# The last output tile of a hybrid trunk: 256 tokens at once, or two halves of 128 with a scale of their own

## The chip, the cores and the metric

The kernel runs on one core of one Trainium2 chip. The metric is the device time of one execution in microseconds. A kernel is run several times, and the median counts.

## The reference

One layer of a trunk for 256 tokens and 2048 features: a gated recurrent branch, a gated short convolution, a merge, then a squared-ReLU MLP and a final RMSNorm. The change touches the MLP and the final norm only:

```
h2 = _rmsnorm(x, g2)
u = jnp.square(jax.nn.relu(jnp.einsum("bsd,df->bsf", h2, w_mlp1)))
x = x + jnp.einsum("bsf,fd->bsd", u, w_mlp2)
...
return _rmsnorm(x, final_g)      # x * rsqrt(mean(x*x) + 1e-6) * g
```

## The kernel before

Everything lies with features on the 128 partitions and tokens along the free axis. The tile `x` is [128, 16, 256]: 16 tiles of 128 features by 256 tokens. Every float32 operand of a matmul is split into two parts of the type fp32r, a high one and a low one, and a product is made of three terms: high weight by high and low activation (one matmul of 512 columns, since the two activation parts lie side by side), and low weight by high activation (one of 256 columns). `product` (L226 on) issues these pairs at L232 and L233, 8 to a slab of weights.

Weights stream in as slabs of [128, 1024]. `Weights.make` loads a slab by a DMA from the SP queue (L61), rounds it on ScalarE into `whi` (L63) and makes `wlo` as the difference on VectorE (L64). `Weights.take` keeps three slabs ahead; four buffers of each kind exist, so the rounding of a slab waits until TensorE is done with the slab four before it.

The MLP has 8192 hidden features and runs in two passes `h` of 4096. In a pass, 32 tiles of `u` are made (L380: squared ReLU, then `split`, L133 and L134), and then 16 output tiles, each of 4 slabs, or 32 pairs (L387 on). The second RMSNorm is not applied ahead of the first matrix: its factor `rs` (1 / mean square, since the ReLU is squared) multiplies the output tiles at L389. In the second pass each tile is also squared and added to `ssq` (`squares`, L190 and L191) and multiplied by the final gain (L395).

The last tile of the second pass (`flat`) has three matmuls of 256 columns per row block in place of the pair (L228 to L230), all into one half of a PSUM tile, so that no addition of two halves follows. Then come L389 and L390, the squares of this tile (L397), the gain (L398), and `rsqrt` (L156): two matmuls with a matrix of ones (L154) put the sum over features on every partition, for 256 tokens; ScalarE takes a square root (L161), VectorE a reciprocal (L164) and one Newton step (L165 to L167), all on [128, 256]. Six products (L403) scale the 16 tiles, and after each a DMA (L404) stores [128, n, 256], on the SP queue or on ScalarE's.

Each engine works its instructions in the order in which they are issued; a framework inserts the semaphores.

Of the kernel before, what the change touches and what calls it, by code (L numbers as in the profile page):

```python
# [14 lines left out]
P = 128  # L15
# [9 lines left out]
AHEAD = 300  # L25

PARAMS = [("g1", NT), ("g2", NT), ("gf", NT), ("b_in", 7 * NT), ("ca_w", 4 * NT), ("ca_b", NT),
          ("br", NT), ("bi", NT), ("lam", NT), ("cb_w", 3 * NT), ("one", 1)]
OFF = {}
_n = 0  # L30
for _name, _w in PARAMS:
# [5 lines left out]


class Weights:
    """Streams [128, ncol] slabs of weights and splits each exactly into two fp32r parts."""  # L40

    def __init__(self, tc, raw_pool, hi_pool, lo_pool, slabs):
        self.tc, self.nc, self.slabs = tc, tc.nc, slabs
# [41 lines left out]
def trunk(ctx: ExitStack, tc: tile.TileContext, xT, par, w_in, w_lru, w_pa, w_pb, w_o, w_1, w_2, out):  # L85
# [43 lines left out]
        return pr[:, OFF[name] + j:OFF[name] + j + 1]  # L129

    def split(dst, src):
        """dst [P, 2, S] fp32r <- src as two parts."""
        nc.scalar.copy(dst[:, 0, :], src)  # L133
        nc.vector.tensor_tensor(dst[:, 1, :], src, dst[:, 0, :].bitcast(F32), ALU.subtract)  # L134

# [12 lines left out]
    ssq = keep.tile([P, S], F32, name="ssq")  # L148

    def total(parts):  # L150
        """PSUM [P, S]: the sum over partitions and parts, on every partition."""
        ps = psl.tile([P, 512], F32, name="psl")
        for i, sq in enumerate(parts):
            nc.tensor.matmul(ps[:, :S], ones, sq, start=i == 0, stop=i == len(parts) - 1)  # L154
        return ps[:, :S]

    def rsqrt(dst, parts):
        """dst [P, S] <- 1 / sqrt(mean of the squares + EPS)."""
        ps = total(parts)
        y = wk.tile([P, S], F32, name="t")  # L160
        nc.scalar.activation(y, ps, AF.Sqrt, scale=1.0 / D, bias=eps)  # L161
        m = wk.tile([P, S], F32, name="low")
        nc.vector.tensor_scalar(m, ps, 1.0 / D, EPS, ALU.mult, ALU.add)
        nc.vector.reciprocal(y, y)  # L164
        nc.vector.tensor_tensor(m, m, y, ALU.mult)  # L165
        nc.vector.scalar_tensor_tensor(m, m, -0.5, y, ALU.mult, ALU.mult)
        nc.vector.scalar_tensor_tensor(dst, m, 1.5, y, ALU.add, ALU.mult)  # L167
# [14 lines left out]
    nc.sync.dma_start(pr[:, NT:], par[:, NT:])  # L182

    def squares(src, j):
        """ssq, by partition, of the tiles up to j."""
        if j == 0:
            nc.scalar.activation(ssq, src, AF.Square)
        else:
            sq = wk.tile([P, S], F32, name="s")
            nc.scalar.activation(sq, src, AF.Square)  # L190
            nc.vector.tensor_tensor(ssq, ssq, sq, ALU.add)  # L191
# [5 lines left out]
    s2 = keep.tile([P, NT], F32, name="s2")  # L197

    def decay():
        """s4 <- -4 softplus(-lam)."""  # L200
        nc.scalar.activation(s2, lam, AF.Abs)
        nc.scalar.activation(sg, s2, AF.Sigmoid, scale=-1.0)
        nc.vector.tensor_scalar(sd, sg, -1.0, 2.0, ALU.mult, ALU.add)
        nc.vector.reciprocal(sd, sd)
        nc.vector.tensor_tensor(sg, sg, sd, ALU.mult)
        nc.vector.tensor_tensor(s2, sg, sg, ALU.mult)
        nc.vector.tensor_scalar(sd, s2, 1.0 / 17, 1.0 / 15, ALU.mult, ALU.add)
        for n in (13, 11, 9, 7, 5, 3, 1):
            nc.vector.tensor_tensor(sd, sd, s2, ALU.mult)
            nc.vector.tensor_scalar(sd, sd, 1.0 / n, None, ALU.add)  # L210
        nc.vector.tensor_tensor(sd, sd, sg, ALU.mult)
        nc.vector.tensor_scalar(s2, lam, -1.0, 0.0, ALU.mult, ALU.max)
        nc.vector.scalar_tensor_tensor(s2, sd, 2.0, s2, ALU.mult, ALU.add)
        nc.vector.tensor_scalar(s4, s2, -4.0, None, ALU.mult)

    def product(acts, k0, nh, flat=False):
        """PSUM [P, 2, S]: the sum of its two halves, or if flat its first half, is the next weights' product
        with acts."""
        ps = psz.tile([P, 2, S], F32, name="psz")
        n = nh * HALF  # L220
        for c in range(nh):
            hi, lo = W.take()
            for k in range(HALF):
                a = acts(k0 + c * HALF + k)
                i = c * HALF + k
                if flat:  # L226
                    w = slice(k * P, (k + 1) * P)
                    nc.tensor.matmul(ps[:, 0, :], hi[:, w], a[:, 0, :], start=i == 0, stop=False)  # L228
                    nc.tensor.matmul(ps[:, 0, :], hi[:, w], a[:, 1, :], start=False, stop=False)  # L229
                    nc.tensor.matmul(ps[:, 0, :], lo[:, w], a[:, 0, :], start=False, stop=i == n - 1)  # L230
                    continue
                nc.tensor.matmul(ps, hi[:, k * P:(k + 1) * P], a, start=i == 0, stop=False)  # L232
                nc.tensor.matmul(ps[:, 1, :], lo[:, k * P:(k + 1) * P], a[:, 0, :], start=False, stop=i == n - 1)  # L233
        return ps
# [17 lines left out]
        z_done(z_product(), j, dst, func)  # L252

    def first_pair():
        """The products of the first two tiles, side by side, as x and the weights come in."""
        w = W.first(4)
        two = [psz.tile([P, 2, S], F32, name="psz") for _ in range(2)]
        for k in range(NT):
            for m in range(2):
                hi, lo = w[k // HALF * 2 + m]  # L260
                c = slice(k % HALF * P, (k % HALF + 1) * P)
                nc.tensor.matmul(two[m], hi[:, c], xg[:, k], start=k == 0, stop=False)  # L262
                nc.tensor.matmul(two[m][:, 1, :], lo[:, c], xg[:, k, 0, :], start=False, stop=k == NT - 1)  # L263
        return two
# [109 lines left out]
    for h in range(2):  # L374
        u = [(big2 if h == 1 and c == 0 else big).tile([P, NT, 2, S], F32R, name="mg" if h == 1 and c == 0 else "big")
             for c in range(2)]
        for f in range(NF // 2):
            t = added(product(lambda k: xh[:, k], 0, 2))
            v = wk.tile([P, S], F32, name="s")
            nc.vector.scalar_tensor_tensor(v, t, 0.0, t, ALU.max, ALU.mult)  # L380
            split(u[f // NT][:, f % NT], v)
            if h == 0 and f == 0:
                nc.vector.tensor_scalar(rs, total([ssq]), 1.0 / D, EPS, ALU.mult, ALU.add)
                nc.vector.reciprocal(rs, rs)
        for j in range(NT):
            flat = h == 1 and j == NT - 1
            ps = product(lambda k: u[k // NT][:, k % NT], 0, 4, flat)  # L387
            t = wk.tile([P, S], F32, name="t") if flat else added(ps)
            nc.vector.tensor_tensor(t, ps[:, 0, :] if flat else t, rs, ALU.mult)  # L389
            nc.vector.tensor_tensor(x[:, j, :], x[:, j, :], t, ALU.add)  # L390
            if h == 1 and j < NT - 1:
                squares(x[:, j, :], j)
                if j == NT - 2:
                    nc.scalar.activation(sink, ssq[:, 0:1], AF.Sqrt)
                nc.scalar.activation(x[:, j, :], x[:, j, :], AF.Copy, scale=pc("gf", j))  # L395
    last = wk.tile([P, S], F32, name="s")
    nc.scalar.activation(last, x[:, NT - 1, :], AF.Square)  # L397
    nc.scalar.activation(x[:, NT - 1, :], x[:, NT - 1, :], AF.Copy, scale=pc("gf", NT - 1))  # L398
    rsqrt(rs, [ssq, last])
    at = 0  # L400
    for n in (3, 4, 4, 3, 1, 1):
        c = slice(at, at + n)
        nc.vector.tensor_tensor(x[:, c, :], x[:, c, :], rs1.broadcast_to([P, n, S]), ALU.mult)  # L403
        (nc.sync if at < 3 or at % 2 == 1 and at != 7 else nc.scalar).dma_start(out[:, c, :], x[:, c, :])  # L404
        at += n


def _slabs(w):
    """[K, N] -> [N / 128, K / 1024, 128, 1024]: per 128 columns and 1024 rows, one slab with the rows' low
    index on the partitions."""  # L410
    k, n = w.shape
    w = w.reshape(k // (HALF * P), HALF, P, n // P, P)
    return np.ascontiguousarray(w.transpose(3, 0, 2, 1, 4)).reshape(n // P, k // (HALF * P), P, HALF * P)


def _cols(v):
    """[..., n * 128] -> [128, ... * n]."""
    return np.asarray(v).reshape(-1, P).T


# [28 lines left out]
```

## Time and profile before

| what | value |
|---|---|
| median of 3 runs | 1669.2 us |
| lowest and highest run | 1667.7 and 1669.64 us |
| the profiled execution's span, first to last instruction | 1667.7 us |
| mean granted TensorE clock of the core | 0.996 |
| TensorE busy over the span | 1645.6 us, 99% |
| stores of the output, the two of 384 KB | 2.6 us to landing |

The profiled execution took 1667.7 us, its span, as long as the lowest of the three runs. The views used below are the page of the profile, the timeline (start, length, engine, line, operation, and in brackets the idle time before it and what ended it), the groups of instructions by line and shape, and tables of windows (busy time and number of instructions of each engine in a stretch, then the granted TensorE clock as a share of full speed, the busy share of the 16 DMA engines, and what they moved in GB/s).

### The profile page before, as it was taken

The page shows a single profiled execution, that of the slowest core. Times are in us where ns is not written, and L with a number is a line of the kernel's source. Part 1 is how long each engine was busy: PE and PEld are TensorE (multiplying, and loading weights), DVE is VectorE, ACT ScalarE, POOL GpSimd, SP SyncE. Part 2 cuts the span into 40 slices and gives each one's busy share as a digit, 9 for nine tenths or more (in the row PEclk, how much of TensorE's full clock was granted, in tenths as well). Part 3 has the DMA queues.
Part 4 walks back from the last instruction along what each step waited for, and adds up shares of the span by engine and source line. Part 5 has one row for each costly group of instructions (what it writes and reads, how often), then busy time and mean ns, then how long its engine had stood idle before and what let it go on. Part 6 is the DMA issues. An engine that isn't in the chain of part 4 may idle for free.

```text
span 1667.7 us, 24308 instructions
## 1 busy us (share of the span) xinstructions
PE 1645.6 (99%) x9450; PEld 1437.3 (86%) x9450; DVE 1124.6 (67%) x1617; ACT 866.4 (52%) x1270; POOL 3.4 (0%) x37
## 2 busy tenths in 40 slices
PE   8999999999999999999999999999999999999996
PEld 6888888888888888888888888888888888888886
DVE  7989778878977665656666666665555666655554
ACT  7666666666665444444445544444443444444442
POOL 0000000000000000000000000000000000000000
PEclk9999999999999999999999999999999999999998
DMA  7555555555556555555555555555555555555552
GB/s 256 177 191 188 189 190 189 186 189 189 185 186 191 189 189 188 185 188 188 188 189 189 179 189 189 190 190 189 187 188 185 188 189 188 189 190 190 188 188 93
DMA packets 88244, 312.15 MB, mean 187 GB/s; under 512 B 9920, under 2 KB 12352, under 8 KB 88128
## 3 DMA queue, kind: packets, MB, share of 16 engines
q1 hardware_dynamic: 87840, 309.93, 56.5%
q8 instruction: 74, 1.21, 0.3%
q10 hardware_dynamic: 288, 0.66, 0.1%
q14 instruction: 42, 0.34, 0.1%
HBM read 308.45 MB, written 2.10 MB: 186 GB/s over the span
## 4 chain that ended last, share of the span: by engine, by line
PE 97%; DVE 1%; DMA 1%; ACT 0%; issue 0%; SPq 0%; DVEq 0%; ACTq 0%
PE psz L232 62%; PE psz L233 32%; DMA raw<-w_in_s 1%; PE psz L262 1%; PE psl L327 0%; PE psl L328 0%; PE psl L326 0%; DVE wlo L64 0%; PE psz L263 0%; PE psz L229 0%; PE psz L230 0%; PE psz L228 0%; DVE x L403 0%; ACT whi L63 0%; PE psl L154 0%
## 5 line engine op out<-in xcount | busy, mean ns | idle before, releaser
L232 PE MATMUL psz<-big,whi 128*128 128x512 f32 x4048 | 1420.9, 394 | 1.0 <-ACT whi L63 0.8
L233 PE MATMUL psz<-big,wlo 128*128 128x256 f32 x4048 | 1130.5, 279 | 0.8 <-DVE wlo L64 0.8
L64 DVE TENSOR_TENSOR wlo<-raw,whi 128x1024 fp32r<-128x1024 f32 (+1 forms) x596 | 714.0, 1201 | 511.7 <-ACT whi L63 510.6
L63 ACT CAST whi<-raw 128x1024 fp32r<-128x1024 f32 (+1 forms) x596 | 614.3, 1032 | 772.5 <-issue 433.5
L232 PEld LDWEIGHTS psz<-big,whi 128*128 128x128 f32 x4048 | 759.2, 188 | 182.8 <-ACT whi L63 1.1
L233 PEld LDWEIGHTS psz<-big,wlo 128*128 128x128 f32 x4048 | 759.3, 188 | 1.1 <-DVE wlo L64 1.1
L232 PE MATMUL psz<-mg,whi 128*128 128x512 f32 x496 | 174.6, 395 | 0.0
L233 PE MATMUL psz<-mg,wlo 128*128 128x256 f32 x496 | 139.0, 281 | 0.0
L232 PEld LDWEIGHTS psz<-mg,whi 128*128 128x128 f32 x496 | 93.0, 187 | 22.1 <-DVE mg L134 0.3
L240 DVE TENSOR_TENSOR t<-psz,low 128x256 f32<-128x256 f32 x255 | 105.7, 417 | 0.0
L233 PEld LDWEIGHTS psz<-mg,wlo 128*128 128x128 f32 x496 | 93.7, 189 | 0.0
L238 ACT COPY low<-psz 128x256 f32<-128x256 f32 x255 | 93.1, 365 | 0.0
L245 DVE TENSOR_TENSOR t<-t,rs 128x256 f32<-128x256 f32 x112 | 47.1, 422 | 2.3
L380 DVE SCALAR_TENSOR_TENSOR s<-t 128x256 f32<-128x256 f32 x64 | 27.2, 425 | 2.1
L338 DVE RECIPROCAL q<-q 128x512 f32<-128x512 f32 x8 | 26.8, 3346 | 0.0
L294 DVE SCALAR_TENSOR_TENSOR xc<-xa,pr,xc 128x256 f32<-128x256 f32 x48 | 22.0, 475 | 0.0
L134 DVE TENSOR_TENSOR big<-s,big 128x256 fp32r<-128x256 f32 x48 | 20.1, 419 | 0.0
L262 PE MATMUL psz<-big,whi 128*128 128x512 f32 x32 | 14.0, 478 | 5.7 <-ACT whi L63 5.7
L133 ACT CAST big<-s 128x256 fp32r<-128x256 f32 x48 | 19.3, 402 | 0.0
L327 PE MATMUL psl<-xs,whi 128*128 128x256 f32 x64 | 18.0, 281 | 0.0
L328 PE MATMUL psl<-xs,wlo 128*128 128x256 f32 x64 | 17.9, 280 | 0.0
L326 PE MATMUL psl<-xs,whi 128*128 128x256 f32 x64 | 17.8, 278 | 0.0
(122 smaller groups left out, 529.4 us busy)
## 6 DMA issues: line engine op xcount, KB each, us to landing
raw<-w_s SPq DMA_DIRECT2D x256, 512.0 KB, 3.5
raw<-w_in_s SPq DMA_DIRECT2D x220, 512.0 KB, 4.2
raw<-w_pb_s SPq DMA_DIRECT2D x32, 512.0 KB, 4.2
raw<-w_pa_s SPq DMA_DIRECT2D x32, 512.0 KB, 4.1
raw<-w_o_s SPq DMA_DIRECT2D x32, 512.0 KB, 3.5
raw<-w_lru_s SPq DMA_DIRECT2D x8, 512.0 KB, 4.0
x<-xT SPq DMA_DIRECT2D x8, 256.0 KB, 4.4
raw<-w_in_s SPq DMA_DIRECT2D x16, 128.0 KB, 4.2
```

The costliest lines, as they stand in the source:

```text
L63: nc.scalar.copy(hi[:, c], raw[:, c])
L64: nc.vector.tensor_tensor(lo[:, c], raw[:, c], hi[:, c].bitcast(F32), ALU.subtract)
L134: nc.vector.tensor_tensor(dst[:, 1, :], src, dst[:, 0, :].bitcast(F32), ALU.subtract)
L232: nc.tensor.matmul(ps, hi[:, k * P:(k + 1) * P], a, start=i == 0, stop=False)
L233: nc.tensor.matmul(ps[:, 1, :], lo[:, k * P:(k + 1) * P], a[:, 0, :], start=False, stop=i == n - 1)
L238: nc.scalar.copy(low, ps[:, 1, :])
L240: nc.vector.tensor_tensor(t, ps[:, 0, :], low, ALU.add)
L245: nc.vector.tensor_tensor(t, t, rs, ALU.mult)
L262: nc.tensor.matmul(two[m], hi[:, c], xg[:, k], start=k == 0, stop=False)
L294: nc.vector.scalar_tensor_tensor(c, xa[:, m, tap:tap + S], pc("ca_w", tap * NT + j), c, ALU.mult, ALU.add)
L338: nc.vector.reciprocal(q, q)
L380: nc.vector.scalar_tensor_tensor(v, t, 0.0, t, ALU.max, ALU.mult)
```

## The change

1. The `flat` form is gone from `product`. The last tile is made by `half(th, between)`, once for tokens 0 to 127 and once for 128 to 255. Each half goes through the same four slabs: 32 pairs of one matmul of 2 x 128 columns (high weights; both activation parts) and one of 128 columns (low weights).
2. The scale of each half is made with tokens on partitions. The squares are the stationary operand and one column of ones the moving one, so the sum lands as [128 tokens, 1]; root, reciprocal and Newton step run on one column. To bring it back to all feature partitions, the identity matrix times the scale (a new parameter `eye`, 128 columns more in the second load of `pr`) is multiplied by ones (`spread`).
3. The matmuls for this stand at chosen places among the pairs: the sum over `ssq` after 16 pairs of the first half and after 20 of the second, the first half's scale after 10 pairs of the second half, its `spread` after 22.
4. The output is [2, 128, 16, 128]; stores move [128, n, 128] (runs of 128 floats in `x`), all on the SP queue: 5, 5, 3, 3 tiles of the first half, then 2, 4, 5, 5 of the second.
5. In the second pass `rs` multiplies `v` ahead of `split` (32 times on [128, 256]) in place of the output tiles (16 times).

```
@@ for f in range(NF // 2):
             nc.vector.scalar_tensor_tensor(v, t, 0.0, t, ALU.max, ALU.mult)
+            if h == 1:
+                nc.vector.tensor_tensor(v, v, rs, ALU.mult)
             split(u[f // NT][:, f % NT], v)
...
-        for j in range(NT):
-            flat = h == 1 and j == NT - 1
-            ps = product(lambda k: u[k // NT][:, k % NT], 0, 4, flat)
-            t = wk.tile([P, S], F32, name="t") if flat else added(ps)
-            nc.vector.tensor_tensor(t, ps[:, 0, :] if flat else t, rs, ALU.mult)
+        for j in range(NT - h):
+            t = added(product(lambda k: u[k // NT][:, k % NT], 0, 4))
+            if h == 0:
+                nc.vector.tensor_tensor(t, t, rs, ALU.mult)
             nc.vector.tensor_tensor(x[:, j, :], x[:, j, :], t, ALU.add)
...
-    rsqrt(rs, [ssq, last])
-    for n in (3, 4, 4, 3, 1, 1):
...
+    def sum_of(th):
+        ps = psl.tile([P, 512], F32, name="psl")
+        nc.tensor.matmul(ps[:, 0:1], ssq[:, th * P:(th + 1) * P], ones[:, 0:1], start=True, stop=False)
+        return ps
+
+    def half(th, between):
+        c = slice(th * P, (th + 1) * P)
+        ps = psz.tile([P, 2, S], F32, name="psz")
+        for k in range(4 * HALF):
+            if k in between:
+                between[k]()
+            hi, lo = w[k // HALF]
+            a = u[k // NT][:, k % NT, :, c]
+            b = slice(k % HALF * P, (k % HALF + 1) * P)
+            nc.tensor.matmul(ps[:, :, :P], hi[:, b], a, start=k == 0, stop=False)
+            nc.tensor.matmul(ps[:, 1, :P], lo[:, b], a[:, 0, :], start=False, stop=k == 4 * HALF - 1)
+        low = wk.tile([P, S], F32, name="low")
+        nc.scalar.copy(low[:, :P], ps[:, 1, :P])
+        xl = x[:, NT - 1, c]
+        nc.vector.tensor_tensor(low[:, :P], low[:, :P], xl, ALU.add)
+        nc.vector.tensor_tensor(xl, ps[:, 0, :P], low[:, :P], ALU.add)
+        sq = wk.tile([P, S], F32, name="s")
+        nc.scalar.activation(sq[:, :P], xl, AF.Square)
+        nc.scalar.activation(xl, xl, AF.Copy, scale=pc("gf", NT - 1))
+        return sq
+
+    def scale_of(th, sq):
+        ps = col[th]
+        nc.tensor.matmul(ps[:, 0:1], sq[:, :P], ones[:, 0:1], start=False, stop=True)
+        r, y, m = (keep.tile([P, 1], F32, name="%s%d" % (n, th)) for n in ("cr", "cy", "cm"))
+        nc.scalar.activation(y, ps[:, 0:1], AF.Sqrt, scale=1.0 / D, bias=eps)
...
+        d = wk.tile([P, S], F32, name="t")
+        nc.vector.tensor_scalar(d[:, :P], eye, m, None, ALU.mult)
+        return d
+
+    def spread(d):
+        ps = psl.tile([P, 1, 512], F32, name="psl")
+        nc.tensor.matmul(ps[:, 0, :P], ones, d[:, :P], start=True, stop=True)
+        return ps[:, :, :P]
+
+    def store(th, by, at, parts):
+        for n in parts:
+            xp = x[:, at:at + n, th * P:(th + 1) * P]
+            nc.vector.tensor_tensor(xp, xp, by.broadcast_to([P, n, P]), ALU.mult)
+            nc.sync.dma_start(out[th, :, at:at + n, :], xp)
+            at += n
+
+    s0 = half(0, {2 * HALF: lambda: begin(0)})
+    s1 = half(1, {10: lambda: by.append(scale_of(0, s0)), 20: lambda: begin(1), 22: store0})
+    store(0, by[0], 10, (3, 3))
+    store(1, spread(scale_of(1, s1)), 0, (2, 4, 5, 5))
```

On TensorE (`psz` is the product's PSUM tile, `psl` that of the small sums, `big` the tile of `u`), the program before ends with the last three of the 96 matmuls of the flat tile and the two sums:

```order
L228 MATMUL psz<-big,whi 128x256
L229 MATMUL psz<-big,whi 128x256
L230 MATMUL psz<-big,wlo 128x256
L154 MATMUL psl<-ssq,ones 128x256
L154 MATMUL psl<-s,ones 128x256
L444 UNCONDITIONAL_BRANCH
```

Now the same place, late in the second half, at its pairs 19 to 23:

```order
L412 MATMUL psz<-big,wlo 128x128
L399 MATMUL psl<-ones,ssq 128x1
L411 MATMUL psz<-big,whi 128x2x128
L412 MATMUL psz<-big,wlo 128x128
L411 MATMUL psz<-big,whi 128x2x128
L412 MATMUL psz<-big,wlo 128x128
L441 MATMUL psl<-t,ones 128x128
L411 MATMUL psz<-big,whi 128x2x128
```

The small matmuls, which stood behind the last product, now stand between its pairs for the first half; those of the second half still stand behind.

On VectorE, at the end of the program, before (from the sum of squares of the last tile but one to the scaled products):

```order
L191 TENSOR_TENSOR ssq<-ssq,s 128x256
L389 TENSOR_TENSOR t<-psz,rs 128x256
L390 TENSOR_TENSOR x<-x,t 128x256
L163 TENSOR_SCALAR low<-psl 128x256
L164 RECIPROCAL t<-t 128x256
L165 TENSOR_TENSOR low<-low,t 128x256
L166 SCALAR_TENSOR_TENSOR low<-low,t 128x256
L167 SCALAR_TENSOR_TENSOR rs<-low,t 128x256
L403 TENSOR_TENSOR x<-x,rs 128x768
L403 TENSOR_TENSOR x<-x,rs 128x1024 x2
```

Now, from the four products of the first half on (`cr`, `cy`, `cm` are the columns of the scale, `pr` holds the identity):

```order
L447 TENSOR_TENSOR x<-x,psl 128x5x128 x2
L447 TENSOR_TENSOR x<-x,psl 128x3x128 x2
L416 TENSOR_TENSOR low<-low,x 128x128
L417 TENSOR_TENSOR x<-psz,low 128x128
L429 TENSOR_SCALAR cr_15888<-psl 128x1
L430 RECIPROCAL cy_15889<-cy_15889 128x1
L431 TENSOR_TENSOR cm_15890<-cr_15888,cy_15889 128x1
L432 SCALAR_TENSOR_TENSOR cm_15890<-cm_15890,cy_15889 128x1
L433 SCALAR_TENSOR_TENSOR cm_15890<-cm_15890,cy_15889 128x1
L435 TENSOR_SCALAR t<-pr,cm_15890 128x128
L447 TENSOR_TENSOR x<-x,psl 128x2x128
L447 TENSOR_TENSOR x<-x,psl 128x4x128
```

The first half's products stand ahead of the second half's additions on this engine, and the operations that make the scale are one column wide.

More of the change, by code (lines that the diff above doesn't have):

```diff
@@ L27 @@
 PARAMS = [("g1", NT), ("g2", NT), ("gf", NT), ("b_in", 7 * NT), ("ca_w", 4 * NT), ("ca_b", NT),
-          ("br", NT), ("bi", NT), ("lam", NT), ("cb_w", 3 * NT), ("one", 1)]
+          ("br", NT), ("bi", NT), ("lam", NT), ("cb_w", 3 * NT), ("one", 1), ("eye", P)]
 OFF = {}
@@ L214, in decay, with product @@
         nc.vector.tensor_scalar(s4, s2, -4.0, None, ALU.mult)
-    def product(acts, k0, nh, flat=False):
+    def product(acts, k0, nh):
         ps = psz.tile([P, 2, S], F32, name="psz")
@@ L225, in product @@
                 i = c * HALF + k
[L226 to L231, printed above, removed]
                 nc.tensor.matmul(ps, hi[:, k * P:(k + 1) * P], a, start=i == 0, stop=False)
@@ L384, in trunk @@
                 nc.vector.reciprocal(rs, rs)
-        for j in range(NT):
-            flat = h == 1 and j == NT - 1
-            ps = product(lambda k: u[k // NT][:, k % NT], 0, 4, flat)
-            t = wk.tile([P, S], F32, name="t") if flat else added(ps)
-            nc.vector.tensor_tensor(t, ps[:, 0, :] if flat else t, rs, ALU.mult)
+        for j in range(NT - h):
+            t = added(product(lambda k: u[k // NT][:, k % NT], 0, 4))
+            if h == 0:
+                nc.vector.tensor_tensor(t, t, rs, ALU.mult)
             nc.vector.tensor_tensor(x[:, j, :], x[:, j, :], t, ALU.add)
-            if h == 1 and j < NT - 1:
+            if h == 1:
                 squares(x[:, j, :], j)
@@ L395, in trunk @@
                 nc.scalar.activation(x[:, j, :], x[:, j, :], AF.Copy, scale=pc("gf", j))
-    last = wk.tile([P, S], F32, name="s")
-    nc.scalar.activation(last, x[:, NT - 1, :], AF.Square)
-    nc.scalar.activation(x[:, NT - 1, :], x[:, NT - 1, :], AF.Copy, scale=pc("gf", NT - 1))
-    rsqrt(rs, [ssq, last])
-    at = 0
-    for n in (3, 4, 4, 3, 1, 1):
[L402 to L405, printed above, removed]
+    w = [W.take() for _ in range(4)]
@@ new lines, in trunk @@
+    eye = pr[:, OFF["eye"]:OFF["eye"] + P]
+    col = {}
+    def sum_of(th):
[22 more added lines that the diff above has]
+        return sq
@@ new lines, in scale_of @@
+    def scale_of(th, sq):
[3 more added lines that the diff above has]
+        nc.scalar.activation(y, ps[:, 0:1], AF.Sqrt, scale=1.0 / D, bias=eps)
+        nc.vector.tensor_scalar(r, ps[:, 0:1], 1.0 / D, EPS, ALU.mult, ALU.add)
+        nc.vector.reciprocal(y, y)
+        nc.vector.tensor_tensor(m, r, y, ALU.mult)
+        nc.vector.scalar_tensor_tensor(m, m, -0.5, y, ALU.mult, ALU.mult)
+        nc.vector.scalar_tensor_tensor(m, m, 1.5, y, ALU.add, ALU.mult)
+        d = wk.tile([P, S], F32, name="t")
+        nc.vector.tensor_scalar(d[:, :P], eye, m, None, ALU.mult)
+        return d
@@ new lines, in spread, with begin @@
+    def spread(d):
[8 more added lines that the diff above has]
+            at += n
+    def begin(th):
+        col[th] = sum_of(th)
@@ L408, in _slabs, with store0 @@
+    by = []
+    def store0():
+        by.append(spread(by.pop()))
+        store(0, by[0], 0, (5, 5))
+    s0 = half(0, {2 * HALF: lambda: begin(0)})
+    s1 = half(1, {10: lambda: by.append(scale_of(0, s0)), 20: lambda: begin(1), 22: store0})
+    store(0, by[0], 10, (3, 3))
+    store(1, spread(scale_of(1, s1)), 0, (2, 4, 5, 5))
 def _slabs(w):
@@ L431 @@
         "par": np.ascontiguousarray(np.concatenate([_cols(v) for v in (
-            norm1_g, norm2_g, final_g, b_in, conv_a_w, conv_a_b, lru_br, lru_bi, lru_lam, conv_b_w, np.ones(P, np.float32))], 1)),
+            norm1_g, norm2_g, final_g, b_in, conv_a_w, conv_a_b, lru_br, lru_bi, lru_lam, conv_b_w, np.ones(P, np.float32), np.eye(P, dtype=np.float32))], 1)),
         "w_in_s": _slabs(np.asarray(w_in)[0]),
@@ L442 @@
     args = [nc.dram_tensor(n, a.shape, mybir.dt.from_np(a.dtype), kind="ExternalInput").ap() for n, a in arrays.items()]
-    args.append(nc.dram_tensor("outT", (P, NT, S), F32, kind="ExternalOutput").ap())
+    args.append(nc.dram_tensor("outT", (2, P, NT, P), F32, kind="ExternalOutput").ap())
     with tile.TileContext(nc) as tc:
@@ L447 @@
     got = r.results[0]["outT"]
-    return np.ascontiguousarray(got.transpose(1, 0, 2).reshape(D, S).T).reshape(1, S, D)
+    return np.ascontiguousarray(got.transpose(0, 3, 2, 1)).reshape(1, S, D)
```

## The prediction

> **What bounds the kernel now.** I read the page first, then the windows of the last stages, then the timeline.
>
> ```profile
> PE 1645.6 (99%) x9450; PEld 1437.3 (86%) x9450; DVE 1124.6 (67%) x1617; ACT 866.4 (52%) x1270; POOL 3.4 (0%) x37
> 1640.00:1652.50 12.50, 12.50 (x104) 12.36 (x103) 3.39 (x6) 3.73 (x6) 0.00 (x0) 1.00 0.01 2
> 1652.50:1667.70 15.20, 1.26 (x6) 0.45 (x4) 8.97 (x13) 1.40 (x3) 0.00 (x0) 0.68 0.36 138
> ```
>
> TensorE (PE) bounds everything up to the end of the last tile. Then it has 1.26 us of work in 15.2 us, and a chain on the other engines sets the end. So two stages count: the last tile, where each added matmul slot is path, and the tail. The tail's chain in the timeline:
>
> ```profile
> 1652.66 0.42 DVE L389 TENSOR_TENSOR t<-psz,rs 128x256 f32<-128x256 f32 x1 [7.15 <-PE psz L230]
> 1653.58 0.42 ACT L397 ACTIVATE s<-x 128x256 f32<-128x256 f32 x1 [6.47 <-DVE x L390]
> 1654.05 0.70 PE L154 MATMUL psl<-s,ones 128*128 128x256 f32 x2 [0.99 <-ACT s L397]
> 1654.79 0.47 ACT L161 ACTIVATE t<-psl,eps 128x256 f32<-128x256 f32 x1 [0.25 <-PE psl L154]
> 1655.63 1.74 DVE L164 RECIPROCAL t<-t 128x256 f32<-128x256 f32 x1
> 1657.41 0.42 DVE L165 TENSOR_TENSOR low<-low,t 128x256 f32<-128x256 f32 x1
> 1658.79 4.77 DVE L403 TENSOR_TENSOR x<-x,rs 128x768 f32<-128x768 f32 x6
> ```
>
> Call E the moment at which the last product is ready: 1652.66. From E to the end are 1667.7 - 1652.66 = 15.04 us: 6.13 until the scale is there (1658.79), 4.77 of products, the rest stores. Dependent steps follow each other about 0.04 us apart (1653.58 + 0.42 to 1654.05). The stores themselves:
>
> ```profile
> 1660.00:1661.00 1.00, 0.00 (x0) 0.00 (x0) 1.00 (x2) 0.00 (x0) 0.00 (x0) 0.50 0.40 160
> 1662.00:1663.00 1.00, 0.00 (x0) 0.00 (x0) 1.00 (x3) 0.00 (x0) 0.00 (x0) 0.50 1.02 410
> 1666.00:1667.00 1.00, 0.00 (x0) 0.00 (x0) 0.00 (x0) 0.00 (x0) 0.00 (x0) 0.50 0.16 54
> ```
>
> A share of 0.40 in the first window puts the first byte at 1660.6, 0.8 us after the first product (953 ns, row below) ended at 1659.75; then the engines are full, about 400 GB/s, until 1666.16. The end follows 1.54 us later. So the 2.1 MB of output, not VectorE (done at 1663.56), end the kernel.
>
> **The slot of a matmul.** The change puts matmuls of 128 columns into the last tile, which no row of before has. What a weight load costs decides their price.
>
> ```profile
> 1640.26 0.39 PE L232 MATMUL psz<-big,whi 128*128 128x512 f32 x1
> 1640.49 0.28 PE L233 MATMUL psz<-big,wlo 128*128 128x256 f32 x1
> 1640.61 0.39 PE L232 MATMUL psz<-big,whi 128*128 128x512 f32 x1
> 1640.96 0.28 PE L228 MATMUL psz<-mg,whi 128*128 128x256 f32 x1
> 1641.08 0.28 PE L229 MATMUL psz<-mg,whi 128*128 128x256 f32 x1
> ...
> 940.44 0.19 PEld L232 LDWEIGHTS psz<-big,whi 128*128 128x128 f32 x1 [0.24 <-DVE big L138]
> 940.44 0.50 PE L232 MATMUL psz<-big,whi 128*128 128x512 f32 x1
> 940.55 0.19 PEld L233 LDWEIGHTS psz<-big,wlo 128*128 128x128 f32 x1
> ```
>
> From start to start, 512 columns take 0.23 us and 256 take 0.12: a slope of 0.11 per 256 columns, which would give 128 columns 0.067. But each matmul has its own weights, loaded while the one before streams. At 940.44 TensorE starts after a wait, with nothing to hide the load: the next load begins 0.11 us later, and this matmul is shown 0.50 long instead of 0.39. Both say that a load takes 0.11 us. A matmul of 128 columns streams in about half of that, so the next load would still run: its slot would be 0.115, hardly less than one of 256. The upper bound is plain float32, which L154 shows: 0.70 us for two passes of 256 columns, that is 0.11 for the load, 0.16 for the end (280 ns of a matmul row less its slot), so about 0.21 a pass. Half the columns make 0.105 a pass; two passes, and the 0.015 by which a slot of 256 columns (0.12) exceeds 0.105, make 0.225 us for 128 columns at that rate. I take 0.115, the nearest row, and keep 0.067 and 0.225 as bounds.
>
> The Trainium skill, page "TensorE: Matmul & The Clock Gate", section "Back-to-back issue gap", gives a sustained 81 ns for matmuls of 128 columns with their own weights; by it the sum below would be about 1.7 us shorter, as it shortens 64 slots by 0.034 us, 2.2 in all, and lengthens the wait below by 0.5. The same sentence gives 131 ns for 512 columns, where this trace has 0.23 us, so I give it little weight here.
>
> **Last tile, term by term.** Before, 96 slots of 0.12 from 1640.96, and E at 1652.66. Now: 64 pairs of 0.12 + 0.115 = 15.04 us. Between them stand three sums of one column (two loads of 0.11 each, 0.66 in all) and one spread (two slots of 0.12): 0.90. The first sum needs `ssq` of tile 14:
>
> ```profile
> 1643.72 0.43 DVE L389 TENSOR_TENSOR t<-t,rs 128x256 f32<-128x256 f32 x1
> 1645.09 0.43 DVE L191 TENSOR_TENSOR ssq<-ssq,s 128x256 f32<-128x256 f32 x1 [0.48 <-ACT s L190]
> ```
>
> L389 is gone from this chain, so L191 ends 0.46 earlier, at 1645.06. TensorE is at pair 16 at 1640.96 + 16 x 0.235 = 1644.72 and waits until 1645.1: 0.38, with all later pairs behind it. The end of the last matmul adds 0.1. **E is then 1640.96 + 15.04 + 0.90 + 0.38 + 0.1 = 1657.4, or 4.7 us later.**
>
> **The tail.** Durations of the new shapes come from rows of the nearest sizes:
>
> ```profile
> L394 ACT ACTIVATE sink<-ssq 128x1 f32<-128x1 f32 x1 | 0.2, 203 | 0.0
> L238 ACT COPY low<-psz 128x256 f32<-128x256 f32 x255 | 93.1, 365 | 0.0
> L190 ACT ACTIVATE s<-x 128x256 f32<-128x256 f32 x29 | 11.8, 406 | 2.3 <-DVE x L390 2.3
> L209 DVE TENSOR_TENSOR sd<-sd,s 128x16 f32<-128x16 f32 x7 | 1.2, 172 | 0.2
> L204 DVE RECIPROCAL sd<-sd 128x16 f32<-128x16 f32 x1 | 0.3, 253 | 0.0
> L403 DVE TENSOR_TENSOR x<-x,rs 128x768 f32<-128x768 f32 x2 | 1.9, 953 | 0.0
> L403 DVE TENSOR_TENSOR x<-x,rs 128x1024 f32<-128x1024 f32 x2 | 2.4, 1218 | 0.0
> ```
>
> On VectorE 256 elements cost 0.42 us and 768 cost 0.953, about 1.04 ns each: 0.29 for 128, 0.55 for 384, 0.69 for 512, 0.82 for 640, and 0.16 for one. A reciprocal takes 253 ns for 16 and 1.74 us for 256, so about 0.16 for one. ScalarE: 0.285 for the copy of 128, 0.305 for the squares, 0.20 for one column.
>
> From E for the second half: copy 0.285, two additions 0.58, squares 0.305; sum on TensorE 0.22 + 0.16; root 0.20; five one-column steps 0.80; identity times scale 0.29; spread 0.11 + 0.21 + 0.16; twelve handoffs of 0.04, 0.48: 3.8 us until the scale is there, against 6.13. Then products of 256, 512, 640 and 640 elements: 0.42 + 0.69 + 0.82 + 0.82, less 0.08 where each overlaps the next (the six of before sum to 5.17 and ran 4.77): 2.5. Last store: 0.8 to the first byte, 327 KB at 400 GB/s 0.82, and 1.54 to the end. **Together 9.45 us instead of 15.04: 5.6 us less.** The first half's 1.05 MB leave earlier. Its products follow the spread at 1655.1 and end at 1657.65; the second half's first addition wants VectorE at E + 0.33 = 1657.7, so it does not wait, but by 0.1 only. The second half's first bytes leave at E + 5.0 = 1662.4; the first half's began near 1656.7 and need 2.6 us.
>
> **Elsewhere.** `rs` ahead of the split adds 32 x 0.43 us on VectorE in the first half of the pass and takes 15 x 0.43 out of the other:
>
> ```profile
> 1310.00:1470.00 160.00, 160.00 (x916) 139.36 (x915) 101.29 (x144) 76.23 (x114) 0.00 (x0) 1.00 0.57 188
> 14.00:16.00 2.00, 2.00 (x13) 1.75 (x12) 1.88 (x6) 2.00 (x7) 0.00 (x0) 1.00 1.04 362
> ```
>
> There VectorE is busy 101 of 160 us and TensorE never waits; the 29 tiles of this stretch add 12 us to 101. This costs nothing; without the cover it would be up to 13.8 us. The identity adds 64 KB to the load of `pr`, issued at 13.9 us, where the DMA engines are full: 64 KB at 320 to 360 GB/s is 0.2 us, which I count whole.
>
> **Sum.** 4.7 - 5.6 + 0.2 = -0.7 us against the profiled 1667.7: 1667.0. The median of before lies 1.5 us above that execution, so I forecast a median of **1668.5 us**, no change: about 0.2% (3.3 us) is what a measurement can tell.
>
> **Rivals.** (1) *Slots of 128 columns at 0.067.* For it: the slope of the two sizes. Against it: the row at 940.44. The 64 slots give back 3.1 us, but pair 16 comes 0.77 earlier and waits that much longer for `ssq`, and VectorE is then late with the first half's products by about 0.5: -1.8, a median of 1666.7.
>
> (2) *Slower: 128 columns at the float32 rate.* No fp32r matmul before is below 256 columns, so nothing in the trace excludes it. Each low-weight slot would be 0.225; 64 x 0.11 = 7.0, less the 0.38 of wait: +6.7, a median of 1675.2. It decides from a slot of about 0.18 us on.
>
> (3) *Stores of 512-byte pieces are slow.* `x` now gives runs of 512 bytes, where before they were 1 KB and more for each partition.
>
> ```profile
> 10.00:20.00 10.00, 10.00 (x52) 8.63 (x51) 8.14 (x22) 9.18 (x24) 0.00 (x0) 1.00 0.99 320
> 1500.00:1640.00 140.00, 140.00 (x802) 122.47 (x801) 79.84 (x100) 65.81 (x87) 0.00 (x0) 1.00 0.55 182
> ```
>
> Against it: loads in pieces of 1 to 2 KB (10 to 20 us) reach 320 at a full share, as those of 4 KB do (182 / 0.55 = 331). If a piece of 512 bytes took as long as one of 1 KB, the rate would halve to 200 GB/s: 1.05 MB from E + 5.0 take 5.2 us, then 1.54: 11.7 instead of 9.45, +2.3, a median of 1670.8. The Trainium skill, page "DMA: Bandwidth & Descriptors", section "Specifications", puts the least transfer for line rate at 512 B, just what these pieces have; by it this rival falls.
>
> (4) *The halves don't overlap.* If pair 10 of the second half comes before the first half's squares (due 1.3 us after its end, against 2.35), TensorE waits: up to 1 us, a median of 1669.5.
>
> **Chances.** Forecast 0.60, (1) 0.14, (2) 0.13, (3) 0.10, (4) 0.03. The range 1666.0 to 1672.5 holds the forecast, (1), (3) and (4), with the errors of a dozen estimated steps (about 1 us), and leaves out (2) and some edges. Faster than 0.2% needs (1) with a shorter tail than I sum: about half of (1) and a little of the forecast, 0.11. Slower: (2) and the upper end of (3), 0.17. The rest, 0.72, is no change.
>
> **What would show it.** In the profile after: starts of successive L411 0.235 us apart (0.19 for (1), 0.345 for (2)); E near 1657.4 and the span's end 9.4 us behind it; L399 waiting about 0.4 us for L191; the DMA engines near 400 GB/s in the last stores and idle between the halves (half that rate for (3)); L426 of the first half with no wait. What would prove me wrong first is the low-weight slot, then a tail step that takes twice its estimate.

## The result, and the profile after

The change made the kernel faster: 1657.47 us, median of 4 runs (1656.65 to 1657.99), against 1669.41 us before, median of 4 runs. The ratio is 0.9928, with an interval of 0.9914 to 0.9942. The forecast was no change, so it was wrong by 11 us. The profiled execution took 1657.99 us, its span is 1656.1 us.

The first view is the page of the profile of the changed kernel: the busy time of each engine, then the costliest group of TensorE's instructions, with `big` as the moving tile, and the same line's group with `mg` (L225 stands where L232 stood).

```profile
PE 1637.5 (99%) x9490; PEld 1440.7 (87%) x9490; DVE 1130.7 (68%) x1645; ACT 867.7 (52%) x1275; POOL 3.4 (0%) x37
...
L225 PE MATMUL psz<-big,whi 128*128 128x512 f32 x4048 | 1407.1, 392 | 1.6 <-ACT whi L63 1.2
...
L225 PE MATMUL psz<-mg,whi 128*128 128x512 f32 x496 | 175.9, 399 | 0.0
```

And the same group on the page of before:

```profile
L232 PE MATMUL psz<-big,whi 128*128 128x512 f32 x4048 | 1420.9, 394 | 1.0 <-ACT whi L63 0.8
```

TensorE has 40 instructions more and is busy 8 us less. The group with `big`, the same 4048 instructions in both kernels, is shown with 392 ns in place of 394.

Next the windows of the changed kernel: a stretch of the first half of the second pass, as the prediction showed it of before; the last tile, from its first matmul to E; and the tail, from E to the end.

```profile
1300.00:1460.00 160.00, 160.00 (x925) 140.78 (x924) 114.41 (x173) 77.59 (x116) 0.00 (x0) 1.00 0.59 190
...
1628.96:1645.27 16.31, 15.94 (x138) 15.64 (x136) 6.24 (x16) 4.97 (x10) 0.00 (x0) 1.00 0.03 9
1645.27:1656.10 10.83, 1.15 (x4) 0.80 (x4) 4.29 (x13) 1.24 (x4) 0.00 (x0) 0.61 0.64 182
```

The last tile now begins at 1628.96, where it began at 1640.96: **12.0 us of the gain lie ahead of everything that the change rewrites.** From there to the end pass 27.14 us (16.31 and 10.83), where before had 26.74 (1667.7 - 1640.96). So the rewritten part lost 0.4 us, and the sum, -11.6, is the difference of the two spans. The first row shows where the 12 us come from: in 160 us in which TensorE never waits, it worked 925 instructions, where before worked 916. The same instructions, with nothing between them, run 1% faster.

The windows of that line alone, the same 240 us of both kernels, say it again (columns: TensorE's busy time with the count of its L232 or L225, then the same of the weight loads; granted clock, DMA share and GB/s). First before, then the changed kernel:

```profile
560.00:800.00 240.00, 240.00 (x687) 128.42 (x687) 1.00 0.58 188
```

```profile
560.00:800.00 240.00, 240.00 (x694) 129.96 (x693) 1.00 0.58 190
```

Call the time from start to start of successive high-weight matmuls the period of a pair. Averaged over a stage, without the waits, it is 350.0 ns before and 346.7 ns after in every stage in which `big` alone moves. In the output projection, where `mg` moves, it is 353.2 and 353.3. Of the 4048 pairs with `big`, 240 belong to the last output tiles, which share their stage with `mg` (350.0 and 350.4 on average there); the other 3808, by 3.3 ns each, are some 12.6 us.

So the lead must grow in the stages of `big` alone and stand still in the output projection. The first and the last pair of the projection, before, then in the changed kernel:

```profile
844.18 0.40 PE L232 MATMUL psz<-mg,whi 128*128 128x512 f32 x1
...
934.40 0.40 PE L232 MATMUL psz<-mg,whi 128*128 128x512 f32 x1
```

```profile
836.98 0.40 PE L225 MATMUL psz<-mg,whi 128*128 128x512 f32 x1
...
927.25 0.40 PE L225 MATMUL psz<-mg,whi 128*128 128x512 f32 x1
```

The lead is 7.2 us at its start and as much at its end. It is 12.2 us at the first pair of the last output tiles (1472.97 against 1460.77).

The tail in the timeline of the changed kernel:

```profile
1645.57 0.29 DVE L416 TENSOR_TENSOR low<-low,x 128x128 f32<-128x128 f32 x1
1645.96 0.29 DVE L417 TENSOR_TENSOR x<-psz,low 128x128 f32<-128x128 f32 x1
1646.29 0.31 ACT L419 ACTIVATE s<-x 128x128 f32<-128x128 f32 x1 [0.75 <-DVE x L417]
...
1646.65 0.38 PE L426 MATMUL psl<-ones,s 128*128 128x1 f32 x2 [1.42 <-ACT s L419]
1647.07 0.26 ACT L428 ACTIVATE cy<-psl,eps 128x1 f32<-128x1 f32 x1
1647.37 0.16 DVE L429 TENSOR_SCALAR cr<-psl 128x1 f32<-128x1 f32 x1 [1.11 <-ACT cy L428]
...
1648.21 0.29 DVE L435 TENSOR_SCALAR t<-pr,cm 128x128 f32<-128x128 f32 x1
...
1648.64 0.77 PE L441 MATMUL psl<-t,ones 128*128 128x128 f32 x2 [1.61 <-DVE t L435]
1649.45 2.48 DVE L447 TENSOR_TENSOR x<-x,psl 128x256 f32<-128x256 f32 x4 [0.95 <-PE psl L441]
```

The scale is there 4.18 us after E (1649.45 - 1645.27), the products end at 1651.93. The stores behind them, in windows of 1 us:

```profile
1648.00:1649.00 1.00, 0.36 (x2) 0.39 (x2) 0.45 (x2) 0.00 (x0) 0.00 (x0) 0.50 0.50 143
1649.00:1650.00 1.00, 0.41 (x2) 0.11 (x1) 0.55 (x2) 0.00 (x0) 0.00 (x0) 0.50 0.00 0
1650.00:1651.00 1.00, 0.00 (x0) 0.00 (x0) 1.00 (x2) 0.00 (x0) 0.00 (x0) 0.50 0.19 55
...
1652.00:1653.00 1.00, 0.00 (x0) 0.00 (x0) 0.00 (x0) 0.00 (x0) 0.00 (x0) 0.50 1.02 279
1653.00:1654.00 1.00, 0.00 (x0) 0.00 (x0) 0.00 (x0) 0.00 (x0) 0.00 (x0) 0.50 0.99 298
1654.00:1655.00 1.00, 0.00 (x0) 0.00 (x0) 0.00 (x0) 0.00 (x0) 0.00 (x0) 0.50 0.64 188
```

The engines are full and move 279 to 298 GB/s. Before, stores in pieces of 3 and 4 KB moved 410 at the same share (1662 to 1663, shown with the prediction), and its last ones, in pieces of 1 KB, something between:

```profile
1665.55:1666.05 0.50, 0.00 (x0) 0.00 (x0) 0.00 (x0) 0.00 (x0) 0.00 (x0) 0.50 1.03 342
```

By the share of the last row, the last byte goes at 1654.64; the end follows 1.5 us later.

### The profile page after: what moved, and what is told of

Read it like the earlier page. It is cut to its first block, busy times and chain, and to the rows that moved or that the text cites. A ratio compares the mean times of both kernels' runs of the same rounds, so it can differ in the third digit from the quotient of the medians.

```text
span 1656.1 us, 24430 instructions
## 1 busy us (share of the span) xinstructions
PE 1637.5 (99%) x9490; PEld 1440.7 (87%) x9490; DVE 1130.7 (68%) x1645; ACT 867.7 (52%) x1275; POOL 3.4 (0%) x37
## 4 chain that ended last, share of the span: by engine, by line
PE 97%; DMA 1%; DVE 1%; ACT 0%; SPq 0%; issue 0%; DVEq 0%; ACTq 0%
PE psz L225 62%; PE psz L226 32%; DMA raw<-w_in_s 1%; DVE wlo L64 1%; PE psz L411 0%; PE psl L319 0%; PE psl L320 0%; PE psl L321 0%; DMA pr<-par 0%; ACT whi L63 0%; PE psz L412 0%; DVE x L447 0%; SPq L61 0%; SPq L172 0%; PE psl L154 0%
## 5 line engine op out<-in xcount | busy, mean ns | idle before, releaser
L225 PE MATMUL psz<-big,whi 128*128 128x512 f32 x4048 | 1407.1, 392 | 1.6 <-ACT whi L63 1.2
L225 PEld LDWEIGHTS psz<-big,whi 128*128 128x128 f32 x4048 | 760.8, 188 | 171.1 <-ACT whi L63 1.6
L225 PE MATMUL psz<-mg,whi 128*128 128x512 f32 x496 | 175.9, 399 | 0.0
L225 PEld LDWEIGHTS psz<-mg,whi 128*128 128x128 f32 x496 | 93.3, 188 | 23.1 <-DVE mg L134 0.2
L233 DVE TENSOR_TENSOR t<-psz,low 128x256 f32<-128x256 f32 x255 | 105.9, 418 | 0.0
L138 DVE SCALAR_TENSOR_TENSOR big<-x,pr,big 128x256 fp32r<-128x256 f32 x32 | 14.7, 481 | 4.7 <-ACT big L137 4.7
L319 PE MATMUL psl<-xs,whi 128*128 128x256 f32 x64 | 17.9, 280 | 0.0
```

The costliest lines, as they stand in the source:

```text
L233: nc.vector.tensor_tensor(t, ps[:, 0, :], low, ALU.add)
```

## The experiments

**The question.** Why do unchanged instructions run faster? What the change alters for them are addresses. The tile `pr` grew by 512 bytes per partition (the identity), and the six columns `cr`, `cy` and `cm` take 32 bytes each, in the pool that lies ahead of the weights. So `raw`, `whi`, `wlo` and `mg` lie 704 bytes further; `big` lies where it was. Theory A: the place of the weights sets the period. Rival B: the new program does it in some other way (its order, its other load on VectorE, its stores). All addresses below are those in the programs.

**1 and 2. The address alone, both ways.** Before gets a tile that nothing uses, 704 bytes long, at the end of the pool that grew; the changed kernel gets one of 320, which brings its addresses back to those of before modulo 1024.

```
+    keep.tile([P, 176], F32, name="pad")   # in the kernel before
+    keep.tile([P, 80], F32, name="pad")    # in the changed kernel
```

> The kernel before with one unused tile of 704 bytes for each partition behind the small tiles, which puts raw, whi, wlo, the work tiles and mg on the very addresses they have after the change (whi at 152544 instead of 151840). Nothing else differs. Theory P (placement): the pairs of matmuls come every 346.7 ns as after the change, not every 350.0, and the time falls by about 11 us, to 1658. Rival Q (something in the edits, such as ScalarE's queue without stores or rs ahead of the split, speeds the whole run): pairs stay at 350.0 and the time stays at 1669.

> The changed kernel with an unused tile of 320 bytes, so that raw, whi, wlo, the work tiles and mg lie 1024 bytes further than in the kernel before, at the same place within any 1024 bytes. Theory P, if the place within 1024 bytes is what counts: pairs at 350.0 ns again, and the time within 1.5 us of the kernel before, since the last tile and the tail together differ by -0.5 us (26.3 us against 26.7 in the two traces). Rival Q: stays at 1657.5.

Before with its weights moved took 1656.5 us (ratio to before 0.9924, 0.9907 to 0.994), and its pairs 346.7 ns. The changed kernel with its weights moved back took 1670.1 us (ratio 1.0006, 0.9997 to 1.0016), and its pairs 350.0 ns. The same window, first of the moved before, then of the changed kernel moved back:

```profile
560.00:800.00 240.00, 240.00 (x693) 129.93 (x693) 1.00 0.58 191
```

```profile
560.00:800.00 240.00, 240.00 (x686) 128.44 (x686) 1.00 0.58 189
```

The gain goes with the addresses, not with the code. B fell. The second run also says what the change does by itself: at the old addresses, nothing that can be measured.

**3 and 4. A simple rule of alignment?** Before, the weights begin 32 bytes past a multiple of 64, and so they do after. If alignment to 64 or 128 bytes mattered, 32 bytes more would help.

```
+    keep.tile([P, 8], F32, name="pad")     # in each of the two kernels
```

> The kernel before with an unused tile of 32 bytes: the weights and mg begin at a multiple of 64 bytes (whi at 151872, 64 past a multiple of 256) instead of 32 past one. Theory P with alignment to 64 bytes as its cause: a pair period clearly below 346.7 ns, and with mg aligned the output projection at the same period as the other stages (353 before). If only the distance to the moving tile counts: something between 340 and 355 without such a rule. Rival Q: 350.0.

> The changed kernel with an unused tile of 32 bytes: whi at 152576, a multiple of 1024, mg at 194560, a multiple of 1024 too. Theory P with alignment to 64 bytes: as short a period as in e3, below 346.7. If a common start of weights and moving tile within some larger block is bad: longer than 350 in the output projection. Rival Q: 346.7 and 1657.5 us.

Both became slower: 1681.23 us and 1674.42 us in one execution each, with pairs of 353.3 and 351.1 ns where `big` moves. The idea of alignment fell: the time depends on the address, but starts at a multiple of 64 bytes, or of 1024, don't make it shorter.

**5 and 6. Which tile?** Before, with a pad ahead and one behind, so that only the weights move (`raw`, `whi`, `wlo`; `mg` and the work tiles keep their place modulo 1024), or only `raw`.

```
+    keep.tile([P, 176], F32, name="pad")
+    padl.tile([P, 80], F32, name="padl")   # behind wlo: the weights alone
...
+    padh.tile([P, 80], F32, name="padh")   # behind raw: raw alone
```

> The kernel before with 704 bytes of padding ahead of the weight buffers and 320 behind them: raw, whi and wlo lie where they do after the change (whi at 152544), while the work tiles and mg keep their old place within 1024 bytes. If the place of the weights counts: 346.7 ns a pair wherever the moving tile is big, 1658 us or so. If the work tiles or mg count: 350.0 ns and 1669 us.

> The same, but the 320 bytes stand behind raw: only the buffers that the loads write and the rounding reads have moved; whi and wlo are at their old place within 1024 bytes. If TensorE's reading of the weights counts: 350.0 ns and 1669 us. If the loads' or the rounding's place counts: 346.7 ns and 1658 us.

The weights alone gave 1654.05 us and 346.7 ns; `raw` alone 1669.53 us and 350.0 ns, beside 1670.83 us for before on that chip (one execution each). The weights alone, then `raw` alone:

```profile
560.00:800.00 240.00, 240.00 (x693) 129.91 (x693) 1.00 0.58 190
```

```profile
560.00:800.00 240.00, 240.00 (x686) 128.43 (x687) 1.00 0.57 188
```

So it is `whi` and `wlo`, TensorE's stationary operands (they moved together; which of the two counts was not tried). In the output projection, where `mg` moves, run 5 had a third period, 348.9 ns: the weights had been moved against `mg`, which stood still. That pointed to the distance between the two operands.

**7. The map.** A kernel of nothing but the pairs of `product` (the products are dropped), with the weights at 32 places and the moving tile at six.

```
+    for m in M_OFFS:
+        for o in W_OFFS:
...
+                nc.tensor.matmul(ps, hi[:, b:b + P], mov[:, a:a + 2 * S], start=i == 0, stop=False)
+                nc.tensor.matmul(ps[:, S:], lo[:, b:b + P], mov[:, a:a + S], start=False, stop=i == PAIRS - 1)
```

> No trunk: only pairs of matmuls as in product (512 columns with a high weight, 256 with a low one), 20 in a row for each of 32 starts of the weights (0 to 992 past a multiple of 1024, in steps of 32) and each of 6 starts of the moving tile, while the other engines and the DMA engines do nothing; the output is x, the result of the products is dropped. If the place alone sets the period: with the moving tile at 128, 350.0 ns with weights at 288, 346.7 at 992, 353.3 at 320 and 351.1 at 0, as in the kernels before, after, e3 and e4. If it takes the other engines' or the loads' traffic: one period for all starts. If only the distance between the two tiles counts: the row for 832 is that for 128, moved by 704.

The period, worked out from the starts of the last 12 pairs of each group, is the same for all six places of the moving tile if it is listed by the start of the weights less that of the moving tile, modulo 256 bytes:

```
distance    0      32     64     96     128    160    192    224
ns        353.3  353.3  353.3  346.7  351.1  350.0  348.9  346.7
```

There are 24 groups for each distance. Two stand apart: the very first of the run, at 128, with 434.8 ns, and one at 192, with 353.3. The other engines were idle from 40 us on, so no contention with them is needed:

```profile
100.00:1300.00 1200.00, 1200.00 (x6847) 1048.92 (x6846) 0.00 (x0) 0.00 (x0) 0.00 (x0) 1.00 0.00 1
```

Before has a distance of 160 to `big` (350.0 ns), the changed kernel 96 (346.7), run 4 has 128 (351.1): all three agree, and so does run 5 with 192 to `mg` (348.9). Run 3 does not: at 192 to `big` it had 353.3, and the map says 348.9, but for that one group. In the output projection before, after and runs 1, 3 and 4 have a distance of 0; before and after had 353.2 and 353.3 ns there, runs 1, 3 and 4 had 346.7 to 346.9.

**8 and 9. The best place for both tiles.** From `mg` the weights still lie at a distance of 0. Another 160 bytes, behind the weights, put it at a distance of 96 as well. Once in the changed kernel, once in before (which gets the 704 bytes too), so that the two are compared at one placement.

```
+    padl.tile([P, 40], F32, name="padl")   # in both
+    keep.tile([P, 176], F32, name="pad")   # in before alone
```

> The changed kernel with 160 bytes of padding ahead of the work tiles, which puts mg (and the work tiles) at 128 past a multiple of 256, as big is; the weights stay at 224. By the map a distance of 96 then holds for every tile that moves: 346.7 ns also in the output projection (353.4 in the changed kernel) and in the last second-matrix stage (350.3 on average): 256 x 6.7 + 480 x 3.6 = 3.4 us less, 1654 us. If mg's place does not count: 1657.5.

> The kernel before with 704 bytes ahead of the weights and 160 ahead of the work tiles: the same places as in e8, every pair at 346.7. The difference of e8 and e9 is then the change alone. By my terms, set right with the trace after (last tile and tail 26.3 us against 26.7), e8 is faster by 0.5 us. If placement is not all, and another edit of the change sped the whole run: e8 faster by several us.

The change took 1652.62 us (ratio 0.9904, 0.9889 to 0.9919), before at that place 1651.95 us (0.9903, 0.9889 to 0.9916). All stages of both have 346.7 ns. Both beat the changed kernel as it stands, and between them nothing can be measured. The first matmul of the last tile, in the timeline of the change, then of before at that place:

```profile
1625.30 0.28 PE L413 MATMUL psz<-mg,whi 128*128 128x256 f32 x1
```

```profile
1625.02 0.28 PE L231 MATMUL psz<-mg,whi 128*128 128x256 f32 x1
```

With spans of 1652.4 and 1651.5 us the rewritten part takes 27.1 us in the one and 26.5 in the other: the change costs 0.6 us there by these two executions, which the times of the runs don't separate. The forecast for run 9, the change 0.5 us ahead, missed the sign. It came from 26.3 us for the last tile and the tail, which stands in the expectations of runs 2 and 9 and is not what the trace after shows: 27.1.

**10. The worst place.** Before with 96 bytes, which puts the weights at 0 from `big` and from `mg`.

```
+    keep.tile([P, 24], F32, name="pad")
```

> The kernel before with 96 bytes of padding: weights and mg at 128 past a multiple of 256, the distance to big and to mg 0, which the map gives 353.3 ns: 3.3 ns more for some 4280 pairs, 14 us, a time of 1683. If the map, made with idle engines, does not hold in the kernel: anything else, 1669 if there is no effect of the place.

It took 1677.16 us: slower, as it should be, but by less than the map says. The windows of L233 show why:

```profile
100.00:500.00 400.00, 380.51 (x1098) 205.15 (x1097) 1.00 0.58 190
560.00:800.00 240.00, 240.00 (x680) 127.66 (x680) 1.00 0.57 187
```

Before has 1088 in the first window and 687 in the second. So the first stage of this kernel runs like the fast ones (346.7 ns from start to start), and the rest at 353.1 to 353.3 ns, with the same distance. Between them stands one wait of TensorE, in the timeline:

```profile
506.33 0.50 PE L233 MATMUL psz<-big,whi 128*128 128x512 f32 x1 [0.35 <-DVE big L134]
```

For 300 us ahead of it the period is 346.7 ns, for 300 us behind it 353.3. At this distance there are two steady periods, and TensorE went from one into the other at this wait. That the wait did it is argued from the one case.

**11 and 12. Two periods.** The pairs alone again, at eight distances, each begun in many ways: in two orders and with four sizes of a float32 matmul ahead; then with a matmul of 256 to 432 columns ahead, or a wait for ScalarE.

```
+    for kick, drained in KICKS:
+        for o in ORDER:
...
+            nc.tensor.matmul(pk[:, :kick], hi[:, o * 8:o * 8 + P], mov[:, M // 4:M // 4 + kick], start=True, stop=True)
```

> Pairs alone as in the first map, the moving tile at 128, the eight distances in two orders, 48 pairs each, with nothing, or one float32 matmul of 1, 37 or 256 columns ahead of each group. If the distance alone sets the period: the same eight periods as in the first map in every group. If a distance has several steady periods, chosen by how the group starts: two values or more for some of them, at 192 above all, where the map had 348.9 and the kernel of e3 353.3. The result of the products is dropped; the output is x.

> The pairs alone again, products dropped, the output wrong. 128 groups of 24 pairs: eight distances (weights minus moving tile, modulo 256), 16 times, and ahead of each group one matmul of 256, 272, ... 432 columns (12 times), then four times a pair of matmuls between which TensorE waits for a copy by ScalarE. So each group begins at another moment relative to the one before. Theory 'the distance sets the period alone': each distance has one period in all 16 rows, as in the first map: 353.3 ns at 0, 32 and 64, 346.7 at 96 and 224, 351 at 128, 350 at 160, 349 at 192. Theory 'some distances have two steady periods, and the start decides': 96 and 224 stay at 346.7 in every row, 128 and 160 within 1 ns of 351 and 350, but 0 and 32 show 346.7 in some rows and 353 in others; and 192 shows 353.3 at least once, as in the kernel whose weights were moved by 32 bytes. If 192 stays at 349 in all rows, that kernel's 353.3 is left open.

How often each period came up, from the starts of each group's second half (in ns; where there are two, the count stands behind):

```
distance        0          32         64     96     128    160    192         224
first, of 8   346.7 (5)  346.7 (3)  353.3  346.7  351.2  350.0  348.9       346.7
              353   (3)  353   (5)
then, of 16   346.7 (6)  346.7 (5)  353.3  346.7  351.1  350.0  348.9 (3)   346.7
              353.3 (10) 353.3 (11)                             353.3 (13)
```

Two groups at 192, in the timeline of run 12, ten pairs from the first row to the second and ten from the third to the fourth:

```profile
283.90 0.40 PE L58 MATMUL psz<-mov,hi 128*128 128x512 f32 x1
...
287.39 0.39 PE L58 MATMUL psz<-mov,hi 128*128 128x512 f32 x1
...
352.37 0.40 PE L58 MATMUL psz<-mov,hi 128*128 128x512 f32 x1
...
355.90 0.39 PE L58 MATMUL psz<-mov,hi 128*128 128x512 f32 x1
```

3.49 and 3.53 us: 349 and 353 ns a pair. So the distances 0, 32 and 192 have two periods each, and which one a group falls into changes with how it begins; the other five have one in every group. This fits run 3 (192, in its other period), run 10, and the output projection at 0 with its 346.7 or 353.3 ns.

## Why the prediction was wrong

**The step that failed is "Elsewhere".** It looked at what the change adds to the stages ahead of the last tile, found it hidden, and kept 1640.96 as the start of the last tile: it took for granted that unchanged instructions keep their period. The runs put in its place: the identity and six columns in front of the weights move these by 704 bytes, the distance from `big` goes from 160 to 96 modulo 256, and each pair with `big` takes 3.3 ns less (346.7 in place of 350.0), 12.0 us by the start of the last tile. What that part said of its own operations held: TensorE worked 160.00 of 160 us, with VectorE at 114.41 (101.29 + 12 was forecast).

The Trainium skill, page "TensorE: Matmul & The Clock Gate", section "Step-by-step: what each phase is for", gives TensorE two independent read ports of SBUF, so that a load of the next weights takes no bandwidth from the running matmul. It names no effect of the place of one against the other, and by that sentence alone none would be expected. In runs 7 and 11 there is one, of up to 6.6 ns a pair with the other engines idle, and the measurement decides; whether bandwidth is the reason, no run shows.

**The local sum was right in its first term and too low in its second.** It gave -0.9 us for the last tile and the tail; they took +0.4.

*The slot of 128 columns*: right. The first pairs of the last tile in the timeline of the changed kernel:

```profile
1629.14 0.33 PE L411 MATMUL psz<-mg,whi 128*128 128x256 f32 x1
1629.31 0.22 PE L412 MATMUL psz<-mg,wlo 128*128 128x128 f32 x1
1629.37 0.33 PE L411 MATMUL psz<-mg,whi 128*128 128x256 f32 x1
1629.54 0.22 PE L412 MATMUL psz<-mg,wlo 128*128 128x128 f32 x1
1629.60 0.34 PE L411 MATMUL psz<-mg,whi 128*128 128x256 f32 x1
```

The weight loads of the same pairs:

```profile
1629.08 0.19 PEld L411 LDWEIGHTS psz<-mg,whi 128*128 128x128 f32 x1
1629.19 0.19 PEld L412 LDWEIGHTS psz<-mg,wlo 128*128 128x128 f32 x1
1629.31 0.19 PEld L411 LDWEIGHTS psz<-mg,whi 128*128 128x128 f32 x1
```

A pair takes 0.23 us (0.235 forecast), and rivals (1), 0.19, and (2), 0.345, fell. The matmuls start 0.17 and 0.06 us apart in turn, and the high-weight one, which follows so closely, is shown 0.05 longer than a matmul of 256 columns is elsewhere (0.28). The loads begin evenly, every 0.115 us or so: the pair goes at the pace of two loads. By the 81 ns that the Trainium skill, page "TensorE: Matmul & The Clock Gate", section "Back-to-back issue gap", gives for 128 columns, a pair would take an estimated 0.20 us (0.12 and 0.081). The trace, with 0.23, does not agree.

*The wait for `ssq`*: right. VectorE's last addition to it, and the sum that needs it:

```profile
1632.62 0.43 DVE L191 TENSOR_TENSOR ssq<-ssq,s 128x256 f32<-128x256 f32 x1 [0.48 <-ACT s L190]
...
1633.10 0.38 PE L399 MATMUL psl<-ones,ssq 128*128 128x1 f32 x2 [0.33 <-DVE ssq L191]
```

0.33 us against 0.38. E came 16.31 us after the start of the tile; 16.44 was forecast (1657.4 - 1640.96).

*The tail*: too short by 1.4 us, 10.83 against 9.45. Three terms were given. The scale took 4.18 in place of 3.8: 0.3 of it is the spread, 0.77 us at a granted clock of 0.50 in place of 0.48 us (the first half's, at 1642.55 and the full clock, took 0.44). The products took 2.48 (2.5 forecast). From their end to the end of the kernel went 4.17 in place of 3.16 us, since the stores are the bound, not the last of them alone: the second half's 1.05 MB left between 1650.8 and 1654.64, in 3.8 us, and not in the 2.6 that 400 GB/s need. So rival (3) was right in kind and half right in size: pieces of 512 bytes went at some 290 GB/s, where it said 200. The stores of before held the hint, 342 GB/s in pieces of 1 KB against 410 in larger ones. By the DMA records of the two traces a piece of 512 bytes takes an engine 28.7 ns on average, one of 1 KB 48.3, of 3 KB 125 and of 4 KB 164: an estimated 10 ns for each piece besides its bytes, by a straight line through the four. That the changed kernel has all its stores on one queue is not the reason, since at 1662 of before one queue alone moved the 410. The Trainium skill, page "DMA: Bandwidth & Descriptors", section "Specifications", puts the least transfer for line rate at 512 B; these rows, with a full share of the engines, do not agree.

*Rival (4)*: fell. The sum for the first half starts without a wait (no bracket in its row of the timeline):

```profile
1639.34 0.33 PE L426 MATMUL psl<-ones,s 128*128 128x1 f32 x2
```

The DMA engines idled between the halves (0.00 at 1649), as forecast.

*The change doing nothing measurable* was the forecast, and at equal addresses it holds (runs 2, 8 and 9). It holds because the terms are small, not because they were right: the changed kernel was 0.7 us behind in runs 8 and 9 and 1.2 in run 2, neither clear of noise, where the sum had it 0.7 ahead. The prediction was of the change as it is built, though, and that brings its addresses along. None of the rivals had that, and the range, 1666.0 to 1672.5, left it out. The trace of before had one hint: the same pair of instructions took 350.0 ns with `big` and 353.2 with `mg`, back to back in both stages.

What stays open is why the period depends on the distance, and why with 256 bytes. No run looked inside the reading of the operands. Nor was it tried whether other shapes or types of matmuls show it. The spread of run 1's executions, 1654.66 to 1658.03 us, fits 496 pairs with `mg` (distance 0) that fall into one period or the other, 6.6 ns apart, 3.3 us in all; that is argued, since one execution of it was profiled (346.7 ns in its projection).

## What to carry to other kernels

An edit that adds or grows a tile moves those behind it, and in a kernel that TensorE bounds this alone can be worth more than the edit: here 12 us by the addresses and nothing that could be measured by the code. So, where TensorE is the bound, judge an edit at equal addresses (a pad of unused bytes gives them back), and read the period of the unchanged matmuls first, as a count in a window where TensorE never waits. Once the tiles are settled, try a few pads: for pairs of this shape a distance of 96 modulo 256 bytes gave 346.7 ns in every group, and in every kernel in the stages where it held for all pairs; 224 did so in the runs of pairs alone.

## What the runs showed of the hardware

- The period of a pair of fp32r matmuls (512 and 256 columns, each with its own weights) depends on the start of the weights less that of the moving tile, modulo 256 bytes: 346.7 to 353.3 ns, 1.9%, with all other engines idle.
- At the distances 0, 32 and 192 the same stream has two steady periods, up to 6.6 ns apart. It holds one for hundreds of microseconds; one change from one to the other, at 506 us of run 10, came at a wait of 0.35 us.
- A matmul of 128 columns behind one of 256, each with its own weights, makes a pair of 0.23 us, as long as two of 256 columns take (0.12 each), and the loads begin every 0.115 us or so.
- Stores in pieces of 512 bytes fill the DMA engines at 279 to 298 GB/s. At the same share, pieces of 1 KB moved 342 and pieces of 3 and 4 KB 410.
